# A decoder block on one core: the normalisation of the two short query tiles moves from GpSimd to ScalarE

## The chip, the cores and the metric

The kernel runs on one core of a Trainium2 chip. Its time is the device time of one execution in microseconds (us), the median over several runs. Lower is better. The engines are TensorE (PE in the profile, its weight loads PEld), VectorE (DVE), ScalarE (ACT), GpSimd (POOL) and SyncE (SP), which only issues DMAs here.

## The reference

One layer of a hybrid decoder block over 512 tokens of width 1024, all in float32. An input projection gives queries, keys and values of 16 heads of width 64. Eight heads do a dilated sliding-window attention, eight a block-sparse one; both add a relative-position bias, and for 512 tokens the kernel does both as a causal softmax over all earlier keys with a bias row of its own per head:

```python
s = q_c @ k.T * scale + bias        # masked where the key is later than the query
p = softmax(s, axis=-1)
o = p @ v
```

The normalised outputs go through `w_out`, then follow a cross-attention over 256 memory tokens, a gated convolution MLP and an output norm.

## The kernel before

Everything is kept feature-major: features on the 128 partitions, tokens on the free axis. A float32 product is run as three passes over operands that are split into a high part (a rounded copy, made on ScalarE) and a low part (the difference, made on VectorE or GpSimd). Weights come as 128x1024 chunks: `split_hi` (L88, ScalarE) and `split_lo` (L97, here on GpSimd for most chunks, later one half on VectorE) prepare them ahead of TensorE.

The self-attention runs over the heads `hh` = 0 to 15 in slots. In slot s TensorE does the scores of head s (`s_steps`), the transposes of the attention weights of head s-1 (`t_steps`) and the output product of head s-2 (`o_steps`), interleaved by the string `ORDER` = "OSOTOSTOST", with projections as fillers in between (`fill`, paced by `PACE`). The order on every engine is that in which the program emits its instructions, and each engine works through its own queue in order. `Later.chain` puts the stages of a chain of operations one step of TensorE apart: `L.step()` is called after each group of matmuls, and stages that are due are emitted there. The order of ScalarE, VectorE and GpSimd is thus fixed by these steps.

The 512 queries of a head are four tiles of 128. Being causal, tile i has 128 (i + 1) keys, so the tiles are 128, 256, 384 and 512 wide; they lie side by side in P (`pt`). `s_steps` takes them as tile 3, tile 2, then the short tiles 0 and 1 together. Each of the three groups has the stages

- a0, L683: VectorE adds the bias, and finds the minimum of each row (a custom operation from PSUM into P);
- a1, L688: ScalarE takes the exponential in place and accumulates the row sums;
- a2, L693 and L695: VectorE takes the reciprocal of the sums, and P is multiplied by it in place, per tile, by the engine that `NME` = "ggvv" names: GpSimd for tiles 0 and 1, VectorE for tiles 2 and 3.

Then `t_steps` transposes P blockwise (L710) in three groups; ScalarE copies each out of PSUM as the high part `pt0h`, `pt1h`, `pt2h` (L249, inside `copy`), and VectorE makes the low parts `pt0l` to `pt2l` (L254, inside `sub`). The first transpose group needs blocks of all four tiles of P. `o_steps` multiplies them with V (L739) into the one PSUM bank "o", which `o_evac` empties through ScalarE (`tmp`) and VectorE (`y`, L760).

The fillers add work to the same queues: the projections of Q and K (VectorE's `tmp`, L257; ScalarE's two copies of half the partitions into `Q` or `K`, L249; the low parts on VectorE and GpSimd, L514, L515, L498), V of the second head group (L251, L261), the memory operands X (`mem_prep`: ScalarE L251, VectorE L261) and the memory's values (`vmh`, `vml`).

`copy` with a scale is a ScalarE activation of the function Copy:

Of the kernel before, what the change touches and what calls it, by code (L numbers as in the profile page):

```python
"""One decoder block on one core, everything kept feature-major (features on partitions, tokens on
the free axis).  Float32 products run as three float32r passes over operands that are split exactly
into a high and a low part."""
# [11 lines left out]
OP = mybir.AluOpType  # L15
# [11 lines left out]
NEG = -1e30  # L27
# columns of the per-feature vectors
C_MIX, C_OUT, C_CROSS, C_MEM, C_FFN, C_FIN, C_CW, C_CB = 0, 8, 16, 24, 32, 40, 48, 48 + 3 * FT
# [9 lines left out]
QKE = "vg"  # L39
NME = "ggvv"  # L40
LOE = "gg"
# [3 lines left out]
GT = (1, 3)  # L45
# softmax storage: query tile i owns columns PO[i] .. PO[i] + 128 (i + 1)
PO = (0, 128, 384, 768)
# [6 lines left out]
class Weights:  # L54
    """Streams 128 x 1024 weight chunks: DMA, then the exact split into float32r parts."""

# [24 lines left out]
    def split_hi(self, part):  # L81
        """One half of the high part of the next chunk."""
        i = self.ns
        if part == 0:
            self.dma(i)
            self.hi[i] = self.pool.tile([P, 1024], F32R, tag="hi", bufs=self.BUFS, name=f"hi{i}")
        a, b = self._parts(i)[part]
        self.nc.scalar.activation(self.hi[i][:, a:b], self.stage[i][:, a:b], AF.Copy)  # L88
        if part == 1:
            self.ns += 1  # L90
# [35 lines left out]
    def tick(self, k):  # L126
        """Works ahead on one chunk while another is consumed; k counts the groups of the latter."""
        if self.hold:
            return
        if k == 0:  # L130
            self.skip_raw()
            ahead = sum(self.chunks[j][1] != "raw" for j in range(self.pos, self.ns))
            self.go = self.ns < len(self.chunks) and ahead < self.BUFS - 1
        if self.go and k in (0, 1):
            self.split_hi(k)
        if self.go and k in (3, 4):
            self.split_lo(k - 3)


class Later:  # L140
    """Emits the stages of a chain of operations some steps of the tensor engine apart."""

# [30 lines left out]
def block_kernel(tc, xT, x_tok, memT, mem_tok, w_in, w_out, w_q, w_km, w_vm, w_o, w_gu, w_dn, vecs, relT, onehot,  # L173
                 addend, out):
    nc = tc.nc
    with ExitStack() as ctx:
# [38 lines left out]

        # ---------------------------------------------------------------- constants and inputs
        vec = perm.tile([P, NVEC], F32, name="vec")
# [41 lines left out]
        def scaled_lo(lo, src, sc, hi):  # L259
            """hi + lo = src * sc, exactly the float32 product (hi is its rounded copy)."""  # L260
            nc.vector.scalar_tensor_tensor(lo, src, sc, bf(hi), op0=OP.mult, op1=OP.subtract)  # L261
# [8 lines left out]
        def square(ssq, src, first):  # L270
            """Square for an elementwise running sum; returns what add() then takes."""
            if first:
                nc.scalar.activation(ssq, src, AF.Square)
                return None
            q = tmp()[:, :src.shape[-1]]
            nc.scalar.activation(q, src, AF.Square)  # L276
            return q
# [5 lines left out]
        def norm_stages(R, ssq, n, d, exact=False):  # L283
            """R = (sum over partitions of ssq / d + eps) ** -0.5 in every partition: a table
            estimate and one Newton step.  R may be ssq."""
            v = {}

            def s0():
                v["h"] = tmp(F32R)[:, :n]
                copy(v["h"], ssq)  # L290

            def s1():
                v["l"] = tmp(F32R)[:, :n]
                sub(v["l"], ssq, bf(v["h"]))

            def s2():
                v["p"] = ps = bank("t")[:, :n]
                if exact:
                    nc.tensor.matmul(ps, ones32, ssq, start=True, stop=True)
                else:  # L300
                    nc.tensor.matmul(ps, ones, v["h"], start=True, stop=False)
                    nc.tensor.matmul(ps, ones, v["l"], start=False, stop=True)

            def s3():
                v["r"], v["a"] = tmp()[:, :n], tmp()[:, :n]
                nc.scalar.activation(v["r"], v["p"], AF.Abs_reciprocal_sqrt, scale=1.0 / d, bias=epsb)
                nc.scalar.activation(v["a"], v["r"], AF.Square)

            def s4():
                a = v["a"]  # L310
                nc.vector.scalar_tensor_tensor(a, v["p"], d * EPS, a, op0=OP.add, op1=OP.mult)
                nc.vector.tensor_scalar(a, a, -0.5 / d, 1.5, op0=OP.mult, op1=OP.add)
                mul(R, a, v["r"])

            return (s2, s3, s4) if exact else (s0, s1, s2, s3, s4)
# [9 lines left out]

        # ---------------------------------------------------------------- bias rows
        scr = dram.tile([NH, 640], F32, name="scr")
# [15 lines left out]
        def load_strip(hh):  # L343
            """strip[p, j] holds 8 * bias at the distance p + j - 127."""
            if hh < NH and hh not in strips:
# [4 lines left out]

        # ---------------------------------------------------------------- V of the dilated heads
        # V[g][t]: keys of token tile t, four heads of hi | lo
        V = {}
# [4 lines left out]
        def v_evac(dst, ps, rc):  # L358
            """ps: [tokens, 4 heads * 64], still to be normalised."""
            src = ps.rearrange("p (j c) -> p j c", j=4)  # L360
            v = dst.rearrange("p (j z c) -> p j z c", j=4, z=2)
            hi, lo = v[:, :, 0, :], v[:, :, 1, :]
            return (lambda: copy(hi, src, rc), lambda: scaled_lo(lo, src, rc, hi))
# [6 lines left out]

        # token statistics from the token-major copies: per-partition sums, then a broadcast row
        def tok_load(src, n):
# [70 lines left out]

        # ---------------------------------------------------------------- projections as fillers
        Q, K, VM = {}, {}, {}
# [103 lines left out]
        def mem_prep(k):  # L549
            """Operands of the memory, into the space of the mixer's operands."""  # L550
            src = VM["st"][k // 4][:, (k % 4) * M:(k % 4) * M + M]
# [78 lines left out]
        def fill(x):  # L630
            """Runs the projections up to the pace that is due at slot x."""
            due = np.interp(x, [a for a, _ in PACE], [b for _, b in PACE])
# [16 lines left out]

        # ---------------------------------------------------------------- self-attention  # L650
        pts = [(ap_.tile([P, 512], F32R, name="pt0h"), ap_.tile([P, 512], F32R, name="pt0l")),
# [6 lines left out]
        def s_steps(hh):  # L658
# [10 lines left out]
            for tiles in ((3,), (2,), (0, 1)):  # L669
# [21 lines left out]
                def a2(parts=parts):  # L691
                    i0, i1 = parts[0][0], parts[-1][0] + 1
                    nc.vector.reciprocal(st[:, 8 + i0:8 + i1], st[:, 4 + i0:4 + i1])  # L693
                    for i, n, src, v in parts:
                        engs[NME[i]].tensor_scalar(v, v, st[:, 8 + i:9 + i], None, op0=OP.mult)  # L695

# [94 lines left out]

        # ---------------------------------------------------------------- w_out, first residual
        L.need(tok["y", 7])
# [11 lines left out]
        def resid(m, ssq, hi, lo, c):  # L805
            """Stages after h[m] is final: operand of the next product, running sum of squares."""
            v = {}
# [35 lines left out]

        # ---------------------------------------------------------------- cross-attention
        R1 = ss1
# [105 lines left out]
        def weave(groups_, at):  # L951
            """Runs the groups of units; at[i]: attention steps before group i."""
            i = 0
# [16 lines left out]

        # ---------------------------------------------------------------- w_o, second residual
        ss2 = rtile("ss2", 0)
# [40 lines left out]

        # ---------------------------------------------------------------- gated convolution MLP
        R2 = ss2
# [56 lines left out]

        # ---------------------------------------------------------------- w_down, last residual, output norm
        ss3 = rtile("ss3", 2)
        R3 = rtile("R3", 3)

        def finish(a, b, prior, sq):
            """Stages of the output norm of tokens a .. b; sq: squares of the last feature tile."""
            R, v = R3[:, a:b], {}
# [68 lines left out]

# [1 line left out]
def _bias_consts():  # L1150
# [16 lines left out]
def _kmaj(w, n):  # L1167
    """[K, n * 128] -> [n, 128 partitions, K / 128 * 128]: one column tile for all k tiles."""
    k = w.shape[0] // P
# [3 lines left out]
def _rows(w, kt, width):  # L1173
    """[1024, C] -> chunks [128, kt k-tiles * width], column group outer, k tiles inner."""
    k, c = w.shape[0] // P // kt, w.shape[1] // width
# [65 lines left out]
```

## Time and profile before

| | |
|---|---|
| time, median of 3 runs | 801.3 us (800.94 to 802.13) |
| profiled execution, first to last instruction | 799.3 us |
| PE busy | 776.4 us, 97% |
| DVE busy | 493.0 us, 62% |
| ACT busy | 389.8 us, 49% |
| POOL busy | 165.2 us, 21% |
| mean granted TensorE clock | 0.990 |

The span runs from the first to the last instruction of the profiled execution; the time of a run also holds what lies around it, some 2 us. Busy time of PE holds pipelined matmuls and does not mean peak rate. Register, branch, semaphore and DMA-issuing instructions are not counted as busy. The granted clock is a share of TensorE's full speed.

### The profile page before, as it was taken

Reading aid. Unit: us, or ns where it says so; the run is one execution under the profiler, and the core shown is the slowest. Engines: PE = TensorE matmul, PEld = TensorE weight load, DVE = VectorE, ACT = ScalarE, POOL = GpSimd, SP = SyncE. Lnnn points to the kernel's source line nnn. Section 1 sums busy time; section 2 is a strip of 40 time slices with the busy share of each in tenths; the row PEclk is TensorE's granted clock in tenths of the full one; section 3 lists DMA queues with packets and bytes.
Section 4 is the critical chain, followed back from the end, with each engine's and each line's share of the span. In section 5 each row is a group of like instructions: output and inputs, shape, how many; then the busy total and the mean of one; then the engine's idle time right before and its main releaser. Section 6 shows DMA issues by size and latency. Waiting matters only on the chain.

```text
span 799.3 us, 10566 instructions
## 1 busy us (share of the span) xinstructions
PE 776.4 (97%) x3916; PEld 657.2 (82%) x3916; DVE 493.0 (62%) x894; ACT 389.8 (49%) x763; POOL 165.2 (21%) x163
## 2 busy tenths in 40 slices
PE   9999999999999998999999999999999999999995
PEld 7878989878898786888888888888888888888884
DVE  4656677678886987666476756666656664332324
ACT  5866666677767533544255533343334343322322
POOL 1056565663645343000021000000000000000001
PEclk9999999999999998999999999999999999999998
DMA  9544243343434222121033332222232233333303
GB/s 346 192 136 138 91 126 93 120 114 122 146 133 155 83 81 104 55 78 53 26 106 106 107 105 101 84 106 95 90 106 105 80 99 99 99 93 98 100 21 105
DMA packets 27107, 85.85 MB, mean 107 GB/s; under 512 B 3072, under 2 KB 5248, under 8 KB 26672
## 3 DMA queue, kind: packets, MB, share of 16 engines
q1 hardware_dynamic: 25696, 83.90, 31.7%
q10 hardware_dynamic: 1232, 1.12, 0.4%
q8 instruction: 30, 0.49, 0.3%
q14 instruction: 21, 0.17, 0.1%
q0 software_dynamic: 128, 0.17, 0.1%
HBM read 78.84 MB, written 2.14 MB: 101 GB/s over the span
## 4 chain that ended last, share of the span: by engine, by line
PE 77%; DVE 12%; ACT 6%; issue 2%; POOL 2%; DVEq 0%; POOLq 0%; ACTq 0%
PE acc L266 15%; PE acc L267 15%; PE acc L268 15%; PE s L266 5%; PE s L267 5%; PE s L268 5%; DVE lo L97 2%; ACT P L688 2%; DVE P L695 2%; PE o L739 1%; DVE tmp L257 1%; DVE P L683 1%; POOL h L832 1%; PE t L710 1%; ACT hi L88 1%
## 5 line engine op out<-in xcount | busy, mean ns | idle before, releaser
L88 ACT ACTIVATE hi<-stage 128x512 fp32r<-128x512 f32 (+1 forms) x264 | 151.7, 616 | 171.6 <-PE acc L267 130.7
L97 DVE TENSOR_TENSOR lo<-stage,hi 128x512 fp32r<-128x512 f32 (+1 forms) x211 | 156.8, 773 | 57.6 <-ACT hi L88 57.5
L266 PE MATMUL acc<-X,hi 128*128 128x512 f32 (+1 forms) x432 | 167.3, 387 | 3.6 <-ACT X L251 3.4
L268 PE MATMUL acc<-X,lo 128*128 128x512 f32 (+1 forms) x432 | 162.9, 377 | 0.0
L267 PE MATMUL acc<-X,hi 128*128 128x512 f32 (+1 forms) x368 | 137.6, 374 | 1.4 <-DVE X L261 1.2
L266 PEld LDWEIGHTS acc<-X,hi 128*128 128x128 f32 x432 | 82.3, 191 | 16.8 <-ACT X L251 3.8
L268 PEld LDWEIGHTS acc<-X,lo 128*128 128x128 f32 x432 | 82.1, 190 | 15.0
L267 PEld LDWEIGHTS acc<-X,hi 128*128 128x128 f32 x368 | 69.8, 190 | 12.6 <-DVE X L261 2.5
L97 POOL TENSOR_TENSOR lo<-stage,hi 128x512 fp32r<-128x512 f32 x53 | 71.6, 1368 | 27.3 <-ACT hi L88 25.7
L266 PE MATMUL acc<-G,hi 128*128 128x512 f32 (+1 forms) x198 | 72.9, 368 | 0.0
L268 PE MATMUL acc<-G,lo 128*128 128x512 f32 (+1 forms) x198 | 72.3, 365 | 0.0
L267 PE MATMUL acc<-G,hi 128*128 128x512 f32 (+1 forms) x198 | 72.3, 365 | 0.0
L266 PE MATMUL s<-X,hi 128*128 128x512 f32 x176 | 68.5, 389 | 0.0
L267 PE MATMUL s<-X,hi 128*128 128x512 f32 x176 | 68.5, 389 | 0.0
L268 PE MATMUL s<-X,lo 128*128 128x512 f32 x176 | 68.5, 389 | 0.0
L688 ACT ACTIVATE P<-P,st 128x512 f32<-128x512 f32 (+1 forms) x64 | 35.6, 557 | 39.9 <-DVE st L683 39.7
L1042 DVE SCALAR_TENSOR_TENSOR c<-a,vec,c 128x512 f32<-128x512 f32 x44 | 33.1, 752 | 24.6 <-ACT c L1037 23.8
L1032 POOL MEMSET a<- 128x2 f32 x22 | 2.1, 100 | 210.3 <-DVE c L1042 210.3
L281 POOL TENSOR_TENSOR ss<-ss,tmp 128x512 f32<-128x512 f32 x14 | 18.2, 1298 | 123.9 <-ACT tmp L276 123.9
L266 PEld LDWEIGHTS acc<-G,hi 128*128 128x128 f32 x198 | 37.3, 188 | 6.2
L267 PEld LDWEIGHTS acc<-G,hi 128*128 128x128 f32 x198 | 37.3, 188 | 6.1
L268 PEld LDWEIGHTS acc<-G,lo 128*128 128x128 f32 x198 | 37.3, 188 | 5.9
(242 smaller groups left out, 1516.4 us busy)
## 6 DMA issues: line engine op xcount, KB each, us to landing
stage<-in_w_gu_dram SPq DMA_DIRECT2D x44, 512.0 KB, 3.3
stage<-in_w_in_dram SPq DMA_DIRECT2D x23, 512.0 KB, 3.4
stage<-in_w_dn_dram SPq DMA_DIRECT2D x16, 512.0 KB, 3.5
strip<-scr SPq DMA_DIRECT2D x16, 256.0 KB, 3.6
stage<-in_w_km_dram SPq DMA_DIRECT2D x8, 512.0 KB, 3.9
stage<-in_w_vm_dram SPq DMA_DIRECT2D x8, 512.0 KB, 3.3
stage<-in_w_out_dram SPq DMA_DIRECT2D x8, 512.0 KB, 3.2
stage<-in_w_q_dram SPq DMA_DIRECT2D x8, 512.0 KB, 3.2
```

What stands on the lines that cost most here:

```text
L88: self.nc.scalar.activation(self.hi[i][:, a:b], self.stage[i][:, a:b], AF.Copy)
L97: self.lo_eng[part].tensor_sub(self.lo[i][:, a:b], self.stage[i][:, a:b], bf(self.hi[i][:, a:b]))
L257: nc.vector.tensor_mul(dst, a, b)
L266: nc.tensor.matmul(ps, wh[:, w0:w0 + P], xh, start=first, stop=False)
L267: nc.tensor.matmul(ps, wh[:, w0:w0 + P], xl, start=False, stop=False)
L268: nc.tensor.matmul(ps, wl[:, w0:w0 + P], xh, start=False, stop=last)
L281: eng.tensor_add(ssq, ssq, q)
L683: nc.vector.tensor_tensor_reduce(v, src, sb[:, :n][:, ::-1], -0.125, 3e38, OP.add, OP.min, accum_out=st[:, i:i + 1])
L688: nc.scalar.activation(v, v, AF.Exp, scale=-1.0, bias=st[:, i:i + 1], accum_out=st[:, 4 + i:5 + i])
L695: engs[NME[i]].tensor_scalar(v, v, st[:, 8 + i:9 + i], None, op0=OP.mult)
L710: nc.tensor.transpose(ps[:, c * P:(c + 1) * P], pt[:, PO[i] + kb * P:PO[i] + (kb + 1) * P], ident)
L1042: nc.vector.scalar_tensor_tensor(v["c"], v["a"][:, 6 + o:6 + o + S], col(C_CW + o * FT + f), v["c"], op0=OP.mult, op1=OP.add)
```

## The change

Stage a2 no longer reads `NME`. The tiles 0 and 1 are scaled in place by `copy`, so on ScalarE, with the reciprocal as the per-partition scale; tiles 2 and 3 stay on VectorE. The constant `NME` and comments go.

```diff
-NME = "ggvv"
...
                     i0, i1 = parts[0][0], parts[-1][0] + 1
                     nc.vector.reciprocal(st[:, 8 + i0:8 + i1], st[:, 4 + i0:4 + i1])
                     for i, n, src, v in parts:
-                        engs[NME[i]].tensor_scalar(v, v, st[:, 8 + i:9 + i], None, op0=OP.mult)
+                        if i < 2:
+                            copy(v, v, st[:, 8 + i:9 + i])
+                        else:
+                            nc.vector.tensor_scalar(v, v, st[:, 8 + i:9 + i], None, op0=OP.mult)
```

## Rows read from the trace of the kernel before

**Rows 1.** The page: busy us, share of the span, instructions of each engine.

```profile
PE 776.4 (97%) x3916; PEld 657.2 (82%) x3916; DVE 493.0 (62%) x894; ACT 389.8 (49%) x763; POOL 165.2 (21%) x163
```

**Rows 2.** Stretches: us, busy us (instructions) per engine, PEclk, DMA share, GB/s.

```profile
48.00:75.00 27.00, 24.96 (x132) 20.69 (x130) 18.54 (x45) 18.29 (x41) 18.07 (x15) 1.00 0.41 127
75.00:134.00 59.00, 58.92 (x377) 53.17 (x378) 40.58 (x99) 38.70 (x90) 33.67 (x30) 1.00 0.38 112
134.00:202.00 68.00, 64.63 (x352) 54.63 (x351) 49.61 (x122) 48.26 (x112) 36.59 (x32) 0.97 0.39 120
...
214.00:244.00 30.00, 27.64 (x215) 26.32 (x214) 24.16 (x58) 21.20 (x53) 17.80 (x15) 1.00 0.30 107
```

**Rows 3.** Groups by form, 45 to 250 us: busy, mean ns | idle before.

```profile
L695 POOL TENSOR_SCALAR P<-P,st 128x256 f32<-128x256 f32 x16 | 15.2, 953 | 0.0
L695 POOL TENSOR_SCALAR P<-P,st 128x128 f32<-128x128 f32 x16 | 11.6, 722 | 33.4 <-DVE st L693 26.7 <-PE s L678 5.0 <-PE acc L533 1.6
...
L688 ACT ACTIVATE P<-P,st 128x128 f32<-128x128 f32 x16 | 6.3, 397 | 7.2 <-DVE st L683 7.2
...
L251 ACT ACTIVATE X<-stage,vec 128x256 fp32r<-128x256 f32 x8 | 3.5, 496 | 0.0
```

**Rows 4.** Timeline of ScalarE, 184 to 197 us: start, us, instruction.

```profile
188.03 1.71 ACT L251 ACTIVATE X<-stage,vec 128x256 fp32r<-128x256 f32 x4
```

**Rows 5.** Waits of TensorE, 45 to 250 us: total us, times, longest.

```profile
PE t L710 <- POOL P L695: 2.7, 5, 0.8
...
PE acc L588 <- DVE vml L261: 1.5, 1, 1.5
...
PE acc L533 <- POOL lo L97: 0.7, 1, 0.7
```

**Rows 6.** The chain that ended last, 48 to 75 us: start, us, what.

```profile
57.06 0.62 ACT K L249
...
66.59 0.53 ACT Q L249
...
73.40 1.54 POOL lo L97
```

**Rows 7.** Timeline round the short tiles of head 8, 152.4 to 154.6 us.

```profile
153.45 0.49 ACT L249 ACTIVATE pt2h<-t 128x384 fp32r<-128x384 f32 x1
...
153.73 1.51 POOL L695 TENSOR_SCALAR P<-P,st 128x128 f32<-128x128 f32 x2 [1.45 <-DVE st L693]
...
153.98 0.56 DVE L254 TENSOR_TENSOR pt2l<-t,pt2h 128x384 fp32r<-128x384 f32 x1 [0.35 <-ACT pt2h L249]
154.45 0.68 DVE L683 CUSTOM_DVE_ANT_0 P<-s,strip 128x512 f32<-128x512 f32 x1
```

**Rows 8.** The chain that ended last, 134 to 202 us.

```profile
141.91 0.38 ACT pt2h L249
...
165.16 0.52 ACT hi L88
...
175.25 0.62 ACT K L249
...
186.73 0.62 ACT Q L249
...
189.64 1.49 DVE X L261
```

**Rows 9.** Timeline of GpSimd and VectorE, 213 to 222 us.

```profile
215.79 0.69 DVE L97 TENSOR_TENSOR lo<-stage,hi 128x512 fp32r<-128x512 f32 x1
215.98 2.13 POOL L695 TENSOR_SCALAR P<-P,st 128x128 f32<-128x128 f32 x2 [0.80 <-DVE st L693]
...
218.08 2.72 POOL L97 TENSOR_TENSOR lo<-stage,hi 128x512 fp32r<-128x512 f32 x2
...
219.57 1.78 DVE L97 TENSOR_TENSOR lo<-stage,hi 128x512 fp32r<-128x512 f32 x1
```

## The prediction

> **What bounds the kernel now.** I read the page first, then the table by stretches, the waits of the tensor engine, the chain that ended last, and the timelines of the queues round the edit. In [rows 1] the reader is to see that TensorE is busy for 97% of the span, so a gain can only be idle time of TensorE that goes away, and a loss can only be idle time that is added. The edit acts while the 16 heads of self-attention run. [Rows 2] cuts that part where the chain changes its character. TensorE is idle for 2.0 us of the first stretch (27.00 - 24.96), for 0.1 us of the second, 3.4 us of the third and 2.4 us of the last. The second has TensorE as its bound. The others do not: there the chain runs through ScalarE and VectorE and touches TensorE only where TensorE stands waiting. ScalarE is busy for 48.3 of the 68 us of the third stretch, 71%, and GpSimd for 36.6.
>
> What TensorE waits for in all of this is in [rows 5]: 2.7 us for GpSimd's part of P, 1.5 us for a `vml`, 0.7 us for a low part from GpSimd. (This counts its idle time alone.) The 2.7 us are what the change can remove at first sight.
>
> **What is removed.** 32 instructions on GpSimd, 16 pairs of 0.72 and 0.95 us [rows 3]: 26.8 us of an engine that waits for others most of the time. Nothing on VectorE changes; the reciprocal and the two long tiles stay there.
>
> **What is added.** 32 copies with a scale on ScalarE. The 128x256 one has a near twin, the memory operand's copy with a per-partition scale, at 496 ns; for 128x128 the nearest row is the exponential of the same shape, 397 ns [rows 3]. Four copies in a row take 1.71 us [rows 4] instead of 4 x 0.496 = 1.98, so each starts 0.09 before the one in front has ended. A pair is then done 0.397 + 0.496 - 0.09 = 0.81 us after its start and holds the queue for 0.72 us. Bounds: 0.60 if the 128x128 copy is as much shorter as the overlap allows (0.30 in the queue for each), 0.89 with no overlap.
>
> The P of the two short tiles is thus ready after 0.81 us instead of 1.51 [rows 7], where ScalarE is free. That is 0.7 us early, and 1.3 us early where GpSimd's pair takes 2.13 us [rows 9].
>
> **The new wait.** The copies stand in ScalarE's queue behind the reciprocal on VectorE, which itself stands behind the exponentials on ScalarE. Head 8 shows it [rows 7]: GpSimd got its operands at 153.73, while ScalarE started `pt2h` at 153.45. After the change ScalarE idles until 153.73, copies until 154.54, and starts `pt2h` at about 154.45, 1.0 us later. Behind it `pt2l` on VectorE (153.98) waits for `pt2h`, and behind that in VectorE's order the next head's score reduction (L683, 154.45), which the next exponential needs. So the copies, though nothing needs them early, hold up the next head. Where other ScalarE work stands between the exponentials and the copies (`hi`, `V`, `vmh`), the reciprocal is ready in time and the price is 0.72.
>
> **Stretch by stretch.**
> - 48 to 75 us, heads 0 and 1. The chain passes ScalarE's `K` copy (57.06) and `Q` copy (66.59), both just behind the place of the copies, and ends in GpSimd's low part at 73.40, which TensorE awaits [rows 5, 6]. Twice 0.72: +1.4 us. TensorE gets head 0's P some 0.5 us sooner, but then only waits longer at 75 us.
> - 75 to 134 us, heads 2 to 6. TensorE hides this: 0.1 us idle in 59, and ScalarE idle for 20 us [rows 2]. I take 0. Without that cover it would be 5 x 0.72 to 5 x 1.0, so 3.6 to 5 us.
> - 134 to 202 us, heads 7 to 11. The chain passes, without TensorE for long, ScalarE's `pt2h` (141.91), `hi` (165.16), `K` (175.25) and `Q` (186.73), and ends in the low part of X on VectorE, where TensorE waits [rows 8]. Each of these is the instruction just behind the copies, or one queued right after it. Heads 7, 10 and 11 at 0.72, heads 8 and 9 at 1.0 (their copies meet an unfinished reciprocal): +4.2 us.
> - 202 to 214 us, head 12: I take 0, since TensorE is on the chain again; at most 1.0.
> - 214 to 244 us, heads 13 to 15. Heads 13 and 14 delay `pt2h` by 1.0 and VectorE's next step by some 0.8 (it has other work in front): +1.6. Against it stands a collision. GpSimd's two splits at 218.08 had to wait behind its pair of P, and VectorE's own split at 219.57 then took 1.78 us where the same form took 0.69 at 215.79 [rows 9]. With P gone GpSimd is some 1.5 us ahead and VectorE 0.8 behind, so I take these 1.1 us back. At head 15 TensorE stops waiting for P, about 0.5 us. Together 0, between -0.5 and +2.
>
> The sum is 1.4 + 0 + 4.2 + 0 + 0 = +5.6 us. The profiled span of 799.3 us becomes about 804.9; the median of the runs is 801.3, 2.0 us above that span, so I predict 806.9 us. The 2.7 us of waits for P don't come off: in the stretches where they stand TensorE arrives early at the next late operand.
>
> **A rule that speaks for a gain.** The row first: with GpSimd's multiplications of P running beside it from 215.98, VectorE's split kept its 0.69 us, and it was GpSimd's pair that stretched from 1.51 to 2.13; GpSimd's splits beside it made it 1.78 [rows 7, 9]. The Trainium skill (GPSIMD Engine Reference, section 1, Specifications) says that GpSimd shares its SBUF interfaces with VectorE and contends with instructions that have two SBUF inputs or run in a 2-port mode. By that rule taken flat, 32 instructions fewer on GpSimd would speed VectorE up; by the row only splits are worth moving apart, and the sum stays +5.6.
>
> **The rivals.**
> - *The contention goes (faster).* Taking P off GpSimd lets its splits run earlier in every head where they stand right behind P, and each collision avoided is worth up to 1.78 - 0.69 = 1.1 us. I count one. From six on the chain-bound heads more than the 5.6 us come back; with seven more in all, 5.6 - 7 x 1.1 = -2.1, so 799.2 us. For it: VectorE is on the chain everywhere outside the second stretch. Against it: most splits wait for ScalarE's `hi`, `K` or `Q`, which move back as well. Chance 0.10. This is the way that the skill's sentence would have it.
> - *The idle time of ScalarE swallows the copies.* It is idle for 20 of 68 us in the third stretch [rows 2]; if the chain, which names only the last wait, has slack of 1 us per head there, the cost is 0 and some of the 2.7 us is gained: 798.6 to 802.9, say 801. Chance 0.16.
> - *The cover fails.* The delays of heads 2 to 6 also come through (3.6 to 5 us more), or longer stalls of TensorE bring its clock down: in the third stretch the mean granted clock was already 0.97 [rows 2], so the engine was for a time at 1.2 instead of 2.4 GHz. 5.6 + 4 = 9.6: 811 us. Chance 0.12.
>
> **How the numbers follow.** The forecast has 0.62, with its own range of 803.3 to 809.5 (0.60 to 0.89 us a pair, and the open terms of the last stretch). A measurement of this kernel tells about 0.2%, 1.6 us, from no change. Faster: 0.06 of the first rival, 0.06 of the second, 0.12 together. Same: 0.02, 0.08 and 0.02 of the forecast's low end, 0.12. Slower: 0.76. The range of 801.0 to 811.0 leaves out the faster cases (0.12), a sliver of the unchanged ones (0.02) and the upper half of the last rival (0.06).
>
> **What would show it.** Right: ScalarE has two activations more per head at L249 or L251 of some 0.4 and 0.5 us; GpSimd has no tensor_scalar on P and is 26.8 us less busy; `pt2h` and the next L683 come 0.7 to 1.0 us later in heads 7 to 11; TensorE's waits for P vanish, while those for `y` (L760), X (L261) and the low part at 75 us grow by about as much as the time; everything from 250 us on is only shifted. Wrong: the 134 to 202 us stretch is no longer than before, the collisions of GpSimd's splits with VectorE fall by several, or the copies cost well under 0.3 us each.

## The result, and the profile after

The changed kernel takes 808.0 us (807.46 to 808.88, 4 runs) against 801.3 us: ratio 1.0082, 95% interval 1.0070 to 1.0094, so 6.7 us slower. The prediction was 806.9 us in a range of 801.0 to 811.0. The profiled execution has a span of 806.1 us, 6.8 more than before. One execution of a later experiment, the copies without the wait, took 1102.9 us at a mean granted clock of 0.655 and is left out; it is the one that was profiled, so that experiment has no trace to read.

The page of the changed kernel, busy time per engine, answers to [rows 1]:

```profile
PE 777.5 (96%) x3916; PEld 656.2 (81%) x3916; DVE 490.4 (61%) x894; ACT 400.8 (50%) x795; POOL 138.1 (17%) x131
```

TensorE does the same work. ScalarE has 32 instructions and 11.0 us more, GpSimd 32 instructions and 27.1 us less. The copies, in the groups by form (45 to 260 us), cost what their neighbours in [rows 3] cost:

```profile
L250 ACT ACTIVATE P<-P,st 128x256 f32<-128x256 f32 x16 | 7.9, 496 | 0.0
...
L250 ACT ACTIVATE P<-P,st 128x128 f32<-128x128 f32 x16 | 6.3, 397 | 1.9 <-DVE st L692 1.9
```

(Lines before the edit have a number one lower than in the kernel before, lines after it two higher.) The waits of TensorE, 45 to 260 us, answer to [rows 5], here with two more rows of the kernel before (45 to 250 us) in front:

```profile
PE o L739 <- DVE y L760: 1.5, 3, 0.8
...
PE acc L267 <- DVE X L261: 1.2, 2, 0.8
```

```profile
PE o L741 <- DVE y L762: 5.9, 5, 1.7
PE acc L266 <- DVE X L260: 2.3, 4, 0.8
PE acc L587 <- DVE vml L260: 1.9, 2, 1.6
PE acc L532 <- POOL lo L96: 1.6, 2, 0.9
PE t L712 <- ACT P L250: 0.7, 1, 0.7
```

The waits for P are down from 2.7 to 0.7 us. Those for `y` are at 5.9 (before 1.5), for X at 2.3 (before 1.2), for GpSimd's low part at 1.6 (before 0.7). TensorE waits less for the operand that was speeded up, and more for the ones behind it.

Where the time went is read by pairing the same TensorE instruction in both traces. The first one after GpSimd's late low part starts at 76.48 instead of 74.99 (+1.5), one of V at 132.73 instead of 128.87 (+3.9), the first of head 10's output product at 208.83 instead of 201.24 (+7.6), the transposes of head 15 at 250.77 instead of 243.87 (+6.9). From there to the end it stays at +6.8. So the stretches of [rows 2] lost 1.5, 2.4, 3.7 and won back 0.7 us.

The chain that ended last, in the stretches of [rows 6, 8], now names the copies themselves, head after head:

```profile
66.92 0.69 ACT P L250 x2
...
74.90 1.53 POOL lo L96
...
145.58 0.69 ACT P L250 x2
...
157.77 0.49 ACT P L250
...
170.15 0.49 ACT P L250
...
181.58 0.68 ACT P L250 x2
...
193.41 0.50 ACT P L250
...
197.22 1.49 DVE X L260
```

Heads 1, 7, 8, 9, 10 and 11 are there. Head 0's copies are not, though ScalarE's `K` copy behind them starts at 57.98 instead of 57.06. TensorE doesn't wait for the P of these copies (head 8's transposes start at 159.49, 1.2 us after it is ready); they are on the chain because of what stands behind them in ScalarE's queue. Head 8's timeline, to be held against [rows 7], shows it:

```profile
157.26 0.17 DVE L692 RECIPROCAL st<-st 128x2 f32<-128x2 f32 x1 [0.71 <-ACT P L687]
157.46 0.80 ACT L250 ACTIVATE P<-P,st 128x128 f32<-128x128 f32 x2 [0.23 <-DVE st L692]
158.29 0.49 ACT L248 ACTIVATE pt2h<-t 128x384 fp32r<-128x384 f32 x1
...
158.81 0.56 DVE L253 TENSOR_TENSOR pt2l<-t,pt2h 128x384 fp32r<-128x384 f32 x1 [1.39 <-ACT pt2h L248]
159.28 0.68 DVE L682 CUSTOM_DVE_ANT_0 P<-s,strip 128x512 f32<-128x512 f32 x1
```

ScalarE idles 0.23 us for the reciprocal, copies for 0.80, and VectorE, which had only 0.35 us to wait for `pt2h` before, waits 1.39. The next head's score reduction, which needs neither, comes after it in VectorE's order.

### The profile page after: what moved, and what is told of

Read it like the earlier page. It is cut to its first block, busy times and chain, and to the rows that moved or that the text cites. A ratio compares the mean times of both kernels' runs of the same rounds, so it can differ in the third digit from the quotient of the medians.

```text
span 806.1 us, 10527 instructions
## 1 busy us (share of the span) xinstructions
PE 777.5 (96%) x3916; PEld 656.2 (81%) x3916; DVE 490.4 (61%) x894; ACT 400.8 (50%) x795; POOL 138.1 (17%) x131
## 4 chain that ended last, share of the span: by engine, by line
PE 72%; DVE 12%; ACT 9%; issue 2%; POOL 2%; DMA 1%; DVEq 0%; SPq 0%; POOLq 0%; ACTq 0%
PE acc L265 15%; PE acc L266 15%; PE acc L267 15%; PE s L266 5%; PE s L265 5%; PE s L267 5%; ACT P L687 3%; DVE P L697 2%; DVE lo L96 2%; ACT hi L87 2%; DVE tmp L256 1%; DVE P L682 1%; POOL h L834 1%; PE o L741 1%; ACT X L250 1%
## 5 line engine op out<-in xcount | busy, mean ns | idle before, releaser
L250 ACT ACTIVATE X<-h,vec 128x512 fp32r<-128x512 f32 x24 | 17.2, 721 | 44.6 <-DVE h L842 27.3
```

Source lines behind the costliest of these rows:

```text
L250: nc.scalar.activation(dst, src, AF.Copy, scale=scale)
```

## The experiments

Each ran in five rounds beside the kernel before, whose median was 801.1 to 801.3 us.

**By heads.** The change in its own place, for some heads only; the others stay on GpSimd.

```diff
-                        if i < 2:
+                        if i < 2 and 2 <= hh <= 6:
                             copy(v, v, st[:, 8 + i:9 + i])
                         else:
-                            nc.vector.tensor_scalar(...)
+                            eng = nc.gpsimd if i < 2 else nc.vector
+                            eng.tensor_scalar(...)
```

> The short tiles are scaled on ScalarE for heads 2 to 6 alone, on GpSimd for the others. The prediction let TensorE hide these heads and gives 801.3 us. The trace of the changed kernel shows TensorE's shift against before grow from +1.5 to +3.9 us between 75 and 134 us, so if each head holds up its own stretch, this alone costs 2.4 us: 803.7. If those 2.4 us came only because heads 0 and 1 had already made the chain late, it costs under 0.5: 801.8 at most.

> Heads 7 to 11 alone on ScalarE. Queue theory (a copy holds up the instructions right behind it, and in this stretch they are on the chain): the prediction's +4.2 us, or the +3.7 by which TensorE's shift grows in the trace between 134 and 202 us, so 805.0 to 805.5. Load theory (ScalarE has 11 us more work, and what counts is how much, spread over all 16 heads): 5/16 of 6.7, so +2.1: 803.4.

> The change's place, heads 0 and 1 alone on ScalarE. Queue theory: GpSimd's low part at 75 us comes 1.4 us later, as predicted and as TensorE's shift of +1.5 us at 75 us in the changed kernel shows; nothing later gives it back: 802.5 to 803. If the slack of the next stretch swallows it: 801.3.

> The change's place, heads 12 to 15 alone. The prediction had 0 (-0.5 to +2); TensorE's shift in the changed kernel falls by 0.7 us from 202 us on, so 800.6. If the four runs by heads (0 and 1, 2 to 6, 7 to 11, 12 to 15) add up to the change's 6.7 us, then 0.8 + 4.0 + 1.4 + x = 6.7 gives x = +0.5: 801.8. The same heads two steps later were at 799.6, so their place is worth 1 to 2 us here.

Measured: heads 0 and 1: 802.43 us, ratio 1.0016 (1.0008 to 1.0025). Heads 2 to 6: 802.11, 1.0010 (1.0001 to 1.0019). Heads 7 to 11: 805.32, 1.0047 (1.0034 to 1.0059). Heads 12 to 15: 800.22, 0.9983 (0.9974 to 0.9992).

Heads 7 to 11, five of 16, make 4.0 of the 6.7 us: what counts is where the copies stand, not how many there are, as the queue theory said. Heads 0 and 1 cost their 1.4 alone. Heads 2 to 6 were between the two theories by their time. In their own trace the V instruction at 128.87 is at 131.00 (+2.1), so the delay is their own. Heads 12 to 15 are even a gain.

The medians add up to +5.3 us, not 6.7, but the traces add up. The TensorE instruction that starts at 300.03 us before starts at 306.86 in the changed kernel (+6.8). In the four runs, heads 0 and 1 first and 12 to 15 last, it starts at 301.68, 301.86, 304.22 and 299.33: +1.7, +1.8, +4.2 and -0.7, together +7.0. What differs comes later. Between 300 and 330 us TensorE's clock falls for a while in every one of these traces, but not for equally long: its mean there was 0.89 before, in the changed kernel and in the run of heads 7 to 11, and 0.94 in the other three. Those three win 0.6 to 0.9 us in that stretch. Why the fall was shorter in them is not shown, and that the medians fall short for the same reason is argued. The kernel before and heads 2 to 6 (columns as in [rows 2]):

```profile
300.00:330.00 30.00, 26.38 (x112) 21.00 (x111) 22.01 (x30) 11.68 (x20) 6.95 (x6) 0.89 0.24 85
```

```profile
300.00:330.00 30.00, 25.90 (x111) 20.64 (x111) 22.46 (x31) 11.12 (x19) 7.71 (x6) 0.94 0.25 88
```

**The same copies later.** One more stage of the chain, two steps of TensorE behind the reciprocal:

```diff
+                def a3(parts=parts):
+                    for i, n, src, v in parts:
+                        if i < 2:
+                            copy(v, v, st[:, 8 + i:9 + i])
...
-                tok["p", hh] = L.chain(a0, a1, a2, d=GS[0], gap=GS[1])
+                wait = [lambda: None] * 1
+                tok["p", hh] = L.chain(a0, a1, a2, *wait, a3, d=GS[0], gap=GS[1])
```

> All 16 heads on ScalarE, the same copies, but emitted two steps of TensorE later, so that they stand behind pt2h in every head and behind K or Q in heads 0, 1, 5, 10 and 11. Queue theory: most of the loss goes, 800.5 to 803. Load theory: ScalarE does the same work in the same stretches, so the loss stays: 806.5 to 808.5.

Measured: 801.03 us, 0.9991 (0.9982 to 1.0). All 32 copies are on ScalarE and the whole loss is gone: the load theory falls. Not all of it is won: TensorE waits 4.0 us in all for P now, the longest time 2.0, in heads whose transposes follow soon.

**ScalarE loaded, GpSimd still scaling.**

```diff
                         engs[NME[i]].tensor_scalar(v, v, st[:, 8 + i:9 + i], None, op0=OP.mult)
+                        if i < 2:
+                            copy(ones, ones32, ones32[:, 0:1])
```

> The kernel before, GpSimd still scaling P, with two 128x128 copies more per head on ScalarE in the place where the change puts its copies; they copy ones over ones and wait for nothing, some 0.6 us of the queue per head. Queue theory: the occupation alone costs most of the loss, some 0.6 of 0.72 us in each of the chain-bound heads and no wait for the reciprocal: +3 to +5, 804.3 to 806.3. If the loss comes from the wait for the reciprocal, or from taking P off GpSimd, it stays at 801 to 802.

Measured: 809.67 us, 1.0100 (1.0084 to 1.0115), +8.3 us: more than either theory gave. The sign is that of the queue theory: copies that feed nothing here and hardly wait (0.5 us in all) cost as much as the change. Its waits of TensorE (45 to 265 us) show that P from GpSimd is still awaited, which the change had removed, and a table by stretches shows where the surplus came from (columns as in [rows 2]):

```profile
PE t L712 <- POOL P L695: 3.0, 6, 0.8
```

```profile
250.00:252.00 2.00, 1.44 (x9) 1.22 (x10) 1.75 (x4) 1.14 (x3) 2.00 (x3) 0.92 0.07 23
252.00:254.00 2.00, 2.00 (x11) 2.00 (x10) 0.69 (x1) 0.91 (x2) 0.83 (x1) 0.50 0.12 23
```

After this stall the granted clock was 0.50, TensorE's 1.2 GHz, and between 250 and 256 us its lag behind the kernel before grew from 7.8 to 9.3 us. Without these 1.5 us the run would be 6.8 us behind by its time, as the change is. In the trace it was already at 7.8 where the change stood at 6.9; this 0.9 is not explained.

**The parts of the price.** First the copies without the wait for the reciprocal: they take a fixed column as their scale, so the short tiles aren't normalised. Then no scaling of the short tiles by any engine. Both kernels leave a part of the work out and serve only to tell what it costs.

```diff
-                            copy(v, v, st[:, 8 + i:9 + i])
+                            copy(v, v, col(C_MIX))
```

```diff
-                        if i < 2:
-                            copy(v, v, st[:, 8 + i:9 + i])
-                        else:
+                        if i >= 2:
```

> The changed kernel, but the copies of the short tiles take a fixed per-feature column as their scale in place of the reciprocal (so these tiles are not normalised): they hold ScalarE's queue as long and wait for nothing. The prediction put 0.3 us of wait for the reciprocal on each of heads 8 and 9 and some on others that the chain passes: 0.6 to 2 us less than the change, 806.0 to 807.4. The dummy copies before suggest that the wait costs nothing: 807.7 to 808.3. If the wait were the cause, 803 or less.

> The short tiles are scaled by no engine (left out), everything else as in the change. Nothing is added to ScalarE and GpSimd is rid of P. Queue theory: only TensorE's waits for P (2.7 us before) go, and part of them comes back at the next late operand: 799 to 801. Contention rival (GpSimd's splits run earlier and clear of VectorE): 797 or less. Against the change at 808.0 the difference is what the copies cost on ScalarE.

Measured: 805.5 us, 1.0054 (1.0040 to 1.0068), without the wait; 798.85 us, 0.9974 (0.9965 to 0.9983), without any scaling. So the change is made of three terms: GpSimd and TensorE rid of the slow P, -2.4 us (801.3 to 798.9); ScalarE's queue held by the copies, +6.7 (to 805.5); the wait for the reciprocal, +2.5 (to 808.0). The second agrees with the 6.8 us of the dummy copies, which pay for the place alone. The last is more than expected, but it is a difference of two measurements whose intervals leave it anywhere from 0.8 to 3.7 us. ScalarE's own idle time before the copies in the changed kernel (45 to 260 us: total, times, longest) is nearer the middle of that:

```profile
ACT P L250 <- DVE st L692: 1.9, 8, 0.2
```

In the run without scaling TensorE doesn't wait for P at all, and the gain of 2.4 us (1.5 in the pair of traces, at 300 us) is close to the 2.7 us of [rows 5]. That the one is the other is argued from the sizes. The contention rival's 797 or less did not come.

**On VectorE instead.**

```diff
-NME = "ggvv"
+NME = "vvvv"
```

> The short tiles are scaled on VectorE (all four tiles there), so neither ScalarE nor GpSimd has them. VectorE stands on the chain too, and the two instructions are in front of the low parts and the next head's score reduction; by the 128x384 form's shortest 0.42 us I estimate 0.4 to 0.5 us a pair against 0.72. Queue theory: a loss of about 0.6 of the change's, with P early: 803 to 805.5. If only ScalarE's load matters: 799.5 to 801.

Measured: 806.0 us, 1.0061 (1.0047 to 1.0074). This is slightly beyond the queue theory's range, and far from what an idle ScalarE and GpSimd alone would give: VectorE's queue is a bad place too. Two things stand behind the surplus. The instructions took 0.46 and 0.41 us, so that the price expected for a pair, 0.4 to 0.5, was that of one (groups by form, 45 to 260 us):

```profile
L695 DVE TENSOR_SCALAR P<-P,st 128x128 f32<-128x128 f32 x16 | 7.4, 463 | 0.6
L695 DVE TENSOR_SCALAR P<-P,st 128x256 f32<-128x256 f32 x16 | 6.6, 411 | 0.0
```

And TensorE's clock fell behind a stall, as in the run with the dummy copies (columns as in [rows 2]):

```profile
244.00:248.00 4.00, 1.54 (x13) 1.45 (x13) 3.21 (x9) 1.85 (x7) 1.76 (x2) 1.00 0.33 124
248.00:252.00 4.00, 4.00 (x23) 4.00 (x23) 1.38 (x2) 1.92 (x4) 1.27 (x1) 0.57 0.40 131
```

From 247.5 to 255 us the lag behind the kernel before grew from 3.6 to 5.1 us.

**A better place.** The later stage, for some heads; GpSimd scales the others. The edit is shown against the kernel with all heads later.

```diff
                 wait = [lambda: None] * 1
-                tok["p", hh] = L.chain(a0, a1, a2, *wait, a3, d=GS[0], gap=GS[1])
+                late = (*wait, a3) if hh >= 12 else ()
+                tok["p", hh] = L.chain(a0, a1, a2, *late, d=GS[0], gap=GS[1])
```

> The copies on ScalarE two steps of TensorE later, for heads 12 to 15 alone; GpSimd scales the others as before. In the run with all heads later TensorE's shift fell from +1.8 us at 201 to -0.4 at 316 us, so 2.2 us are to be won there: 799.1. If this fall only gave back what the earlier heads had lost, it is 801.0 to 801.5.

> The copies two steps later for heads 1, 7 and 12 to 15, GpSimd for the rest: heads whose transposes come long after, and near which the run with all heads later was ahead of the kernel before (by 0.4 to 0.8 us each at 75 and 152 us). 798.5 to 799.2 if that adds to the 799.6 of heads 12 to 15; 799.6 if it is given back.

> The copies two steps later for all heads but 0, 5, 9, 10 and 11, where they stood behind K or Q and TensorE then waited for P (shift up by 0.7 to 1.3 us each at 57, 118, 176 and 187 us). Queue theory: the eleven others have room, 798.3 to 799.6. Load theory: eleven heads' copies cost in proportion, 803 or more.

Measured: heads 12 to 15: 799.56 us, 0.9978 (0.9969 to 0.9987). With heads 1 and 7: 799.19, 0.9966 (0.9954 to 0.9978). All but 0, 5, 9, 10 and 11: 798.51, 0.9970 (0.9958 to 0.9981). The last two can't be told apart; both beat the kernel before by 2 to 2.5 us, and eleven heads' copies on ScalarE cost nothing there. Head 8 in the last one, timeline of ScalarE:

```profile
152.78 0.49 ACT L248 ACTIVATE pt2h<-t 128x384 fp32r<-128x384 f32 x1
153.17 0.79 ACT L250 ACTIVATE P<-P,st 128x128 f32<-128x128 f32 x2
153.86 0.62 ACT L87 ACTIVATE hi<-stage 128x512 fp32r<-128x512 f32 x1
154.50 0.72 ACT L687 ACTIVATE P<-P,st 128x512 f32<-128x512 f32 x1
```

The same 0.79 us of copies, now behind `pt2h`; the reciprocal is done 0.2 us before them (at 152.96), and VectorE makes `pt2l` and the next head's scores meanwhile, so the exponential at 154.50 finds its input. Its stretches (columns as in [rows 2]):

```profile
75.00:134.00 59.00, 58.88 (x378) 53.26 (x379) 39.69 (x99) 41.45 (x98) 27.68 (x23) 1.00 0.41 121
134.00:202.00 68.00, 64.20 (x356) 53.82 (x355) 49.29 (x124) 50.22 (x118) 34.83 (x29) 1.00 0.38 114
```

ScalarE is busier in the third stretch than in the changed kernel (50.2 against 46.9 us below), and TensorE is idle for 3.8 us there: little more than the 3.4 before, against 5.6 in the changed kernel.

## Why the prediction was right

The direction and the mechanism were right, and the size nearly: +6.7 us against +5.6. The changed kernel by stretches, against [rows 2]:

```profile
48.00:75.00 27.00, 24.90 (x127) 20.37 (x126) 17.30 (x43) 18.81 (x43) 13.57 (x11) 1.00 0.38 111
75.00:134.00 59.00, 56.68 (x353) 50.07 (x353) 38.02 (x95) 41.05 (x98) 27.53 (x21) 1.00 0.38 116
134.00:202.00 68.00, 62.41 (x341) 51.70 (x339) 45.22 (x111) 46.94 (x112) 26.11 (x20) 1.00 0.32 97
...
214.00:244.00 30.00, 29.69 (x238) 28.91 (x236) 24.51 (x64) 22.36 (x55) 9.68 (x8) 1.00 0.38 127
```

- *Price of a pair.* 0.81 us forecast (its terms, 0.397 + 0.496 - 0.09, make 0.80), 0.80 measured, 397 and 496 ns each.
- *Heads 0 and 1.* +1.4 forecast, +1.5 in the trace, +1.4 alone.
- *Heads 2 to 6.* This term failed. Forecast was 0, because TensorE was idle for only 0.1 us there; the second row now has 2.3 us, and the chain, which went through TensorE alone here before, names the copies of heads 3, 4 and 5. A TensorE that never waits shows that nothing was late, not by how much it was early. One wait for `y` of 1.06 us (at 116.92) and one for a V of 0.5 make most of the loss of 2.4. (The rest of the 2.3 is a wait of 0.7 for a low part at 76.48; the kernel before has the same one at 74.99, on the other side of the edge.) The loss is half to two thirds of what the prediction had set for the cover gone (3.6 to 5), so its third rival came true in part. Alone these heads cost +1.8 at 300 us, and +0.8 by the medians, with the shorter fall of the clock.
- *Heads 7 to 11.* +4.2 forecast, +3.7 in the trace, +4.0 alone. The steps can be followed in VectorE's score reductions: the one of head 7's 384 keys starts at 137.95 instead of 134.28 (+3.7), head 8's first at 147.16 instead of 142.79 (+4.4, so 0.7 for head 7's copies; 0.72 forecast), head 9's first at 159.28 instead of 154.45 (+4.8). In between, head 8's exponentials are back at +3.8 (156.24 instead of 152.44), so head 8's copies cost 1.0 as forecast. The 0.6 us came back from a collision that I hadn't counted: with P gone, GpSimd's splits were over at 147.20, and VectorE's scaling of the 512-wide tile took 0.49 us where it had taken 1.06 beside them. The timelines of VectorE and of GpSimd, first of the kernel before (140 to 150 us):

```profile
144.56 1.06 DVE L695 TENSOR_SCALAR P<-P,st 128x512 f32<-128x512 f32 x1
```

```profile
142.79 2.54 POOL L97 TENSOR_TENSOR lo<-stage,hi 128x512 fp32r<-128x512 f32 x2
```

Then of the changed kernel, VectorE from 145 to 150 us and GpSimd from 140 to 150 us:

```profile
148.93 0.49 DVE L697 TENSOR_SCALAR P<-P,st 128x512 f32<-128x512 f32 x1
```

```profile
144.67 2.53 POOL L96 TENSOR_TENSOR lo<-stage,hi 128x512 fp32r<-128x512 f32 x2
```

- *Heads 12 to 15.* 0 forecast (-0.5 to +2), -0.7 in the trace, -0.8 alone. The collision of [rows 9] is gone as forecast (0.68 at 227.38 instead of 1.78), but the split that GpSimd now starts early collides at 223.09 for 0.5 us, where VectorE had time. Timeline of the changed kernel, 219 to 232 us:

```profile
222.44 1.30 POOL L96 TENSOR_TENSOR lo<-stage,hi 128x512 fp32r<-128x512 f32 x1
...
223.09 1.19 DVE L96 TENSOR_TENSOR lo<-stage,hi 128x512 fp32r<-128x512 f32 x1
...
227.38 0.68 DVE L96 TENSOR_TENSOR lo<-stage,hi 128x512 fp32r<-128x512 f32 x1
```

- *The wait for the reciprocal.* Mis-sized: in the sum it stands for heads 8 and 9 at 0.28, so 0.6 us, against 2.5 (0.8 to 3.7) by the runs. A wait took 0.23 us, but ScalarE idles for it in 8 heads: in 8 and 9, in 13 and 14 as forecast, and also in 2, 3, 4 and 12, which the sum had at nothing.
- *The gain that doesn't come off.* In the sum P's earlier arrival was worth 0.5 us, at head 15. By the run without scaling it is worth 2.4 us by itself; in the change it is covered by the later delays. That the total is nearer than its parts is in part luck. By stretches, the +2.4 of heads 2 to 6 stands against -0.5 and -0.7 in the two terms behind them; by parts, a gain and a wait that were each taken 1.9 us too small cancel.
- *The rule that spoke for a gain.* Taken flat, the rule of the Trainium skill (GPSIMD Engine Reference, section 1, Specifications) on the interfaces that GpSimd and VectorE share would have had GpSimd's scaling slow VectorE's instructions with two inputs in SBUF. The trace doesn't show that: between 45 and 250 us, four of VectorE's splits of 128x512 ran beside GpSimd's scaling alone in the kernel before and took 0.68 to 0.69 us, as those beside an idle GpSimd did. Taking the scaling away altogether gave 2.4 us, about the size of TensorE's waits for P; a gain beyond that isn't seen. The runs agree with the row's reading: it is beside GpSimd's two-input splits that VectorE's instructions were long (1.06 instead of 0.49 us, 1.78 instead of 0.69).

## What to carry to other kernels

With engines that work through their queues in order, the price of a moved instruction is not its duration on a less busy engine but what stands behind it there and who waits for that: the same copies cost 6.7 us in one place and nothing two steps later, and with eleven heads' copies there and the other five heads' on GpSimd the kernel gains 2.5 us. Put work whose result is needed late behind work that others wait for, above all if it waits for another engine itself. An engine without idle time says nothing of the slack of those that feed it; read that from how early its operands are.

## What the hardware showed unexpectedly

TensorE's clock doesn't simply follow its idle time. Before, it was granted 0.97 on average in the third stretch; in the changed kernel, with 5.6 instead of 3.4 us idle there, it was 1.00 throughout. (That fall, at 193 to 197 us, cost the kernel before nothing by the end of the stretch: the changed kernel is 7.6 us behind it at 189.77 and again at 201.24.) In the run with the dummy copies it fell to 0.50, 1.2 GHz, shortly before 252 us, after TensorE had been busy for 2.68 of 4 us and then 1.44 of 2; the changed kernel had 2.42 of 4 us there, then 2.00 of 2, and kept 1.00. A fall of the clock was worth up to 1.5 us in these runs, as much as some of the effects that were measured: before two close times are compared, the granted clocks have to be.
